# Where three block products of a cross-attention output projection accumulate, and where their weights and the rows behind them are split

## The chip, the cores and the metric

The kernel runs on one core of a Trainium2 chip. The metric is the device time of one execution in microseconds (us); lower is better. The engines that matter here are TensorE (PE in the profile; PEld is its weight load), VectorE (DVE), ScalarE (ACT), GpSimd (POOL) and SyncE (SP), whose queue issues all transfers between device memory and the on-chip memory, SBUF. PE writes its results into PSUM, eight banks of 128 x 512 floats.

## The reference

The kernel computes one layer of an encoder trunk on 1024 tokens of 1024 channels: a mixer (window attention and a gated delta rule side by side), a cross-attention into 256 memory tokens, and a SwiGLU feed-forward. Every sub-layer is wrapped in two RMS norms. What the change touches is the end of the cross-attention and the way into the feed-forward:

```python
    o = jnp.einsum('bhqk,bkhd->bqhd', p, v).reshape(b, s, D_MODEL).astype(h.dtype)
    return o @ w_o
...
        x = x + _rms_norm(c, g_cross_post[l])
        f = _swiglu(_rms_norm(x, g_ffn_pre[l]), w_gate_up[l], w_down[l])
```

All data are float32. A product is made to nearly that precision from three passes: each operand is split into a high part, in the form that PE multiplies at its fast rate (fp32r), and a low part, the rest; PE then adds up high x high, high x low and low x high.

## The kernel before

**Seven products in place of eight.** The projection `o @ w_co` is cut into 2 x 2 blocks: the tokens into a first and a second half of 512, the inner channels into two halves, the output channels into LO and HI. With sums and differences of blocks prepared beforehand, seven block products give the four output blocks (Winograd's form of Strassen's method). One block product is 512 x 512 x 512: 4 tiles of 128 tokens (t), 4 slices of 128 inner channels (k), three passes, so 48 matmuls of 128 x 128 by 128 x 512, all at line 1254 (`three`). `block_product` (line 1256) loops over k outside and t inside and keeps four PSUM banks open.

In order of the program the products are: 1 and 2 into banks A (their sum is the first rows' LO half, copied to `c11`; product 1 alone is kept as `e_`); 3 and 4 into banks Y (`y7 = e_ + Y` in between, `zv = e_ + Y` behind); 5, `part` times b22, into banks X; 6, `s1_` times b11, and 7, `s4_` times a block of w_co, into banks Z. `zv` and `za` are the LO and HI halves of the second rows (together `zl`), `zz` holds the first rows. Before products 6 and 7 the loops are turned: t outside, k inside, so that a tile of rows is complete at every quarter of a product and its finish can begin.

**Weights.** `load_w` (line 119) takes a tile `wraw` from a ring of two, loads it on SP's queue, and splits it into `whi` and `wlo`, two more rings of two: ACT casts the high part (line 103), DVE or POOL subtracts for the low part (line 104). The ring serves all weights of the kernel; the feed-forward's first weights follow those of product 7 in it. `weight_part` (line 1237) splits blocks that are already in SBUF into tiles `wpart`. `part` is a pair of tiles with the split left operand of product 5.

**Finishing a row tile.** `finish` (line 1281), for each of the eight tiles of 128 tokens: load the residual from `d_x1` (SP), the mean square (DVE), its power -0.5 (POOL, 1291), residual added (DVE, 1292), store to `d_x2` (SP), square (ACT, 1295), rstd (POOL, 161 and 162), normalised row (ACT 1299 or DVE 1301, in turn). The adds that take a product from PSUM are at line 1318, the squares at 1279, the multiplications by the gain at 1321 (POOL for LO, DVE for HI).

**Turning the rows.** The feed-forward wants channels in partitions, so PE transposes the normalised rows (line 1379), four 128 x 128 blocks into one bank. For the second half's rows (`first_rows`, in `zl`; the feed-forward takes them first), ACT copies the turned block with its gain from PSUM to `raw` (1390), then ACT casts the high part and DVE subtracts the low part, both from `raw` (1391): `x1h`, `x1l`. The other rows (`last_rows`) are turned the same way and combined with `raw` into four sums T1 to T4 (1402 to 1411). Meanwhile the first four feed-forward blocks run their products on `x1h` and `x1l` alone (1431 to 1447, the matmuls at 1424 under the name pA); the main loop (from 1518) needs T1 to T4.

**What sets the order.** The program is written in one order, and a planner orders each engine's instructions by a simulated time: whatever is ready, the earliest in the program first. Instructions under `high_priority(AHEAD)` count as 300 places earlier; all splits of weights and of left operands do. On the chip each engine then runs its list strictly in that order, and SP's queue too. A tile's memory is given on when its last reader is done: `e_` shares its memory with the first half of `x1h`, `part` with the second halves of `x1h` and `x1l`, and `xr45` (two residual tiles) with the first half of `x1l`.

Of the kernel before, what the change touches and what calls it, by code (L numbers as in the profile page):

```python
# [10 lines left out]
F32 = mybir.dt.float32  # L11
# [65 lines left out]
def tile_hybrid_block(  # L77
# [16 lines left out]
    def f32(ap):  # L94
        return ap.bitcast(F32)
# [1160 lines left out]
    def block_product(banks, a, b_, first=True, last=True, extra=None):  # L1256

        for k in range(HK):
            if k % 2 == 0:
                ah, al = act_part(a, k)  # L1260
            if isinstance(b_, tuple):
                if k % 2 == 0:
                    rows, c0 = (HK * b_[0] + k) * P, HALF * b_[1]
                    wh, wl = load_w(w_co[rows:rows + 2 * P, c0:c0 + HALF], 2, HALF)
                dh, dl = wh[:, k % 2], wl[:, k % 2]
            else:
                dh, dl = weight_part(b_, k)
            for t in range(4):
                three(banks[t], ah[:, k % 2], al[:, k % 2], dh, dl, slice(t * P, (t + 1) * P), first and k == 0,
                      last and k == HK - 1, first and last)  # L1270
            if extra:
                extra(k)
# [33 lines left out]
    def four(spec):  # L1306
        return [p_.tile([P, HALF], F32, tag=t_, name="pst") for p_, t_ in spec]
# [31 lines left out]
    for t in range(4):  # L1339
        square_of(c11[:, t], 0, t)  # L1340
        gained(zz[:, t, LO], c11[:, t], LO)
        add(zv[:, t], e_[:, t], Y[t])
    X = four([PX] * 2 + [PN] * 2)
    block_product(X, tuple(part), b22)
    for t in range(4):
        add(zv[:, t], zv[:, t], X[t])
        square_of(zv[:, t], 0, 4 + t)
        gained(zv[:, t], zv[:, t], LO)
        add(za[:, t], y7[:, t], X[t])
        add(e_[:, t], e_[:, t], X[t])  # L1350
    xr45 = opB3.tile([P, 2, D], F32, tag="b30", name="xr45")
    Z = four([PG] * 4)
    acts = [act_part(s1_, k) for k in (0, 2)]
    wts = [weight_part(b11, k) for k in range(HK)]
    for t in range(4):
        for k in range(HK):
            three(Z[t], *(h[:, k % 2] for h in acts[k // 2]), *wts[k], slice(t * P, (t + 1) * P), k == 0, False, False)
        add(za[:, t], za[:, t], Z[t])
        square_of(za[:, t], 1, 4 + t)
        gained(za[:, t], za[:, t], HI, nc.vector)  # L1360
        finish(4 + t, zl[:, t], (nc.scalar, nc.vector)[t % 2])
    acts = [act_part(s4_, k) for k in (0, 2)]
    wts = [load_w(w_co[(HK + k) * P:(HK + k + 2) * P, HI], 2, HALF) for k in (0, 2)]
    for t in range(4):
        for k in range(HK):
            three(Z[t], *(h[:, k % 2] for h in (*acts[k // 2], *wts[k // 2])), slice(t * P, (t + 1) * P), False, k == HK - 1, False)
        add(zz[:, t, HI], e_[:, t], Z[t])
        square_of(zz[:, t, HI], 1, t)
        gained(zz[:, t, HI], zz[:, t, HI], HI, nc.vector)
        finish(t, zz[:, t], (nc.scalar, nc.vector)[t % 2])  # L1370
    LG.close()

    x1h, x1l = operand(opB, "s1")
    X11, X21 = (x1h[:, 0:HK], x1l[:, 0:HK]), (x1h[:, HK:KT], x1l[:, HK:KT])

    def turned_k(parts, k):
        pt = pn.tile([P, 512], F32, tag="pn", name="ptn")
        for j in range(4):
            nc.tensor.transpose(pt[:, j * P:(j + 1) * P], parts(j, k), ident)
        return pt  # L1380
# [5 lines left out]
        return zz[:, j, k * P:(k + 1) * P]  # L1386

    for k in range(KT):
        pt = turned_k(first_rows, k)
        nc.scalar.activation(raw[:, k, :], pt, AF.Identity, scale=gain("ffn", k))  # L1390
        split(x1h[:, k, :], x1l[:, k, :], raw[:, k, :], eng=nc.vector)
    tr = LR2.enter_context(pool("tr", 1, side="right"))
    T2, T4 = (blocks(t) for t in operand(opA, "s0"))
    T1, T3 = (blocks(t) for t in operand(opB, "s2"))
# [363 lines left out]
```

## Time and profile before

| | us |
|---|---|
| median of 3 runs | 1535.39 |
| lowest and highest of them | 1530.17, 1535.72 |
| the profiled execution | 1530.07 |
| its span | 1528.2 |
| PE busy in the span | 1474.8 |
| DVE, ACT, POOL busy | 1110.1, 745.4, 384.5 |
| all 336 matmuls of the seven products, first to last start | 760.1 to 861.4 |

The span is the part of an execution that the profile covers; the time of the execution is a little longer. A row of a timeline gives the start in the span, the length, engine, line, operation, what is written from what, how many such instructions stand together, and in square brackets how long the engine had stood idle before and what released it. One instruction's length overlaps the next one's start a little on every engine; the cost of one in a full queue is the distance of two starts. A matmul of 128 x 128 by 128 x 512 lasts 0.39 us and the next one starts about 0.23 us later (48 in 11.04 us).

### The profile page before, as it was taken

To read this page: it belongs to the slowest core of one execution; us is meant where nothing else is said; L and a number is where in the kernel's file an instruction comes from. 1 tells how busy PE (TensorE), PEld (TensorE's weight loads), DVE (VectorE), ACT (ScalarE), POOL (GpSimd) and SP (SyncE) were. 2 spreads that over 40 slices of the span, in tenths; PEclk is the share of its full clock that TensorE was granted. 3 is DMA by queue.
4 is the path that set the end of the run, shared out by engine and by line. 5 is a ranking of instruction groups with operands and counts; after the bars stand their busy time and mean duration, and the time that the engine had idled before them with its cause. 6 is when DMAs were issued, how large, how long until landed. Compare 5 with 4: busy or idle time off the path is not lost.

```text
span 1528.2 us, 21073 instructions
## 1 busy us (share of the span) xinstructions
PE 1474.8 (97%) x7403; PEld 1236.7 (81%) x7403; DVE 1110.1 (73%) x1802; ACT 745.4 (49%) x1524; POOL 384.5 (25%) x396
## 2 busy tenths in 40 slices
PE   6999999999999899999999898999999999999997
PEld 5888888878999778888888677888888888888786
DVE  6868999787889865535389886686876554696665
ACT  5578821457567663555455773323223332454532
POOL 2020221311346103342100603352434332000021
PEclk9999999999999999999999999999999999999999
DMA  6235585857996674432341454343433333953255
GB/s 208 76 110 147 144 196 148 222 163 204 322 307 207 223 247 161 168 108 60 104 141 42 173 185 121 123 136 111 152 124 108 104 104 112 328 195 97 103 177 167
DMA packets 264166, 241.91 MB, mean 158 GB/s; under 512 B 33768, under 2 KB 203645, under 8 KB 264061
## 3 DMA queue, kind: packets, MB, share of 16 engines
q1 hardware_dynamic: 264061, 240.57, 50.2%
q8 instruction: 58, 0.95, 0.3%
q14 instruction: 47, 0.39, 0.1%
HBM read 171.02 MB, written 66.88 MB: 156 GB/s over the span
## 4 chain that ended last, share of the span: by engine, by line
PE 67%; DVE 11%; DMA 10%; ACT 6%; issue 3%; SPq 2%; POOL 1%; DVEq 0%; POOLq 0%; ACTq 0%
PE pD L1424 8%; PE pE L1424 8%; PE pA L1424 7%; PE pcq L261 6%; PE pmg L1068 6%; PE pdX L1615 6%; PE pg L261 4%; PE pB L1424 4%; PE pst L1254 4%; PE pdA L1615 2%; PE psc L809 2%; PE pdD L1615 2%; DVE acc L286 2%; DMA qr<-d_q 1%; DVE wlo L104 1%
## 5 line engine op out<-in xcount | busy, mean ns | idle before, releaser
L103 ACT CAST whi<-wraw 128x1024 fp32r<-128x1024 f32 x98 | 102.8, 1050 | 155.0 <-issue 38.2
L104 POOL TENSOR_TENSOR wlo<-wraw,whi 128x1024 fp32r<-128x1024 f32 x38 | 93.0, 2448 | 183.9 <-ACT whi L103 179.6
L261 PE MATMUL pg<-hlo,whi 128*128 128x512 f32 x352 | 139.2, 396 | 0.0
L261 PE MATMUL pg<-hhi,whi 128*128 128x512 f32 x352 | 138.6, 394 | 0.1
L261 PE MATMUL pg<-hhi,wlo 128*128 128x512 f32 x352 | 138.2, 393 | 0.0
L1424 PE MATMUL pA<-b,whi 128*128 128x512 f32 x352 | 112.3, 399 | 2.7 <-ACT m L1441 2.7
L104 DVE TENSOR_TENSOR wlo<-wraw,whi 128x1024 fp32r<-128x1024 f32 x60 | 76.0, 1268 | 42.3 <-ACT whi L103 39.8
L1424 PEld LDWEIGHTS pA<-b,whi 128*128 128x128 f32 x352 | 66.4, 191 | 16.7 <-ACT m L1441 3.3
L1615 PE MATMUL pdX<-dhl,whi 128*128 128x512 f32 x264 | 76.1, 390 | 1.5 <-ACT dhl L103 0.8
L261 PEld LDWEIGHTS pg<-hhi,whi 128*128 128x128 f32 x352 | 66.1, 188 | 13.4 <-ACT hhi L103 0.3
L261 PEld LDWEIGHTS pg<-hlo,whi 128*128 128x128 f32 x352 | 66.2, 188 | 12.7
L261 PEld LDWEIGHTS pg<-hhi,wlo 128*128 128x128 f32 x352 | 66.2, 188 | 12.7
L1502 POOL TENSOR_TENSOR act<-act,up 128x512 f32<-128x512 f32 x33 | 49.8, 1510 | 94.1 <-DVE up L1501 62.0
L1424 PE MATMUL pA<-b,wlo 128*128 128x512 f32 x176 | 69.3, 395 | 0.5 <-DVE wlo L104 0.5
L103 ACT CAST whi<-araw 128x1024 fp32r<-128x1024 f32 (+1 forms) x36 | 35.3, 981 | 68.8 <-PE pdX L1615 27.6
L104 DVE TENSOR_TENSOR wlo<-araw,whi 128x1024 fp32r<-128x1024 f32 (+1 forms) x36 | 40.7, 1131 | 35.8 <-ACT whi L103 35.7
L1474 POOL TENSOR_TENSOR sr<-wraw 128x512 f32<-128x512 f32 x22 | 30.5, 1387 | 130.3 <-DMA wraw<-in_w_gate_up_dram 130.3
L286 DVE SCALAR_TENSOR_TENSOR acc<-cp,cols,acc 128x1024 f32<-128x1024 f32 x48 | 62.0, 1294 | 0.1
L1649 POOL TENSOR_SCALAR frs<-sq 128x1 f32<-128x1 f32 x8 | 11.9, 1496 | 195.4 <-ACT jk L1634 194.5
L1615 PEld LDWEIGHTS pdX<-dhl,whi 128*128 128x128 f32 x264 | 49.3, 188 | 12.7 <-issue 1.1
L1475 DVE TENSOR_TENSOR sr<-sr,wraw 128x512 f32<-128x512 f32 x22 | 37.8, 1719 | 28.4 <-POOL sr L1474 28.4
L1424 PE MATMUL pB<-s,s1h 128*128 128x512 f32 x176 | 54.4, 390 | 2.0 <-ACT s1h L103 2.0
(470 smaller groups left out, 4268.0 us busy)
## 6 DMA issues: line engine op xcount, KB each, us to landing
wraw<-in_w_gate_up_dram SPq DMA_DIRECT2D x52, 512.0 KB, 3.9
kv<-d_kv SPq DMA_DIRECT2D x32, 512.0 KB, 7.4
wraw<-in_w_in_dram SPq DMA_DIRECT2D x22, 512.0 KB, 4.3
b<-in_w_down_dram SPq DMA_DIRECT2D x20, 512.0 KB, 8.0
araw<-d_as SPq DMA_DIRECT2D x20, 512.0 KB, 3.7
pz<-d_pz SPq DMA_DIRECT2D x32, 256.0 KB, 7.0
wraw<-in_w_ckv_dram SPq DMA_DIRECT2D x16, 512.0 KB, 5.6
wraw<-in_w_out_dram SPq DMA_DIRECT2D x16, 512.0 KB, 3.6
```

What stands on the lines that cost most here:

```text
L103: nc.scalar.copy(hi, src)
L104: (eng or nc.vector).tensor_tensor(lo, src, f32(hi), ALU.subtract)
L261: nc.tensor.matmul(p_, w[:, k, :], ah[a][:, k, :], start=(k == 0 and i == 0), stop=(k == nk - 1 and i == 2))
L286: nc.vector.scalar_tensor_tensor(acc, cp[:, t:t + S], taps[t], acc, ALU.mult, ALU.add)
L809: nc.tensor.matmul(out[:, d, h, :], lt[:, d, h, :], rt[:, d, h, :], start=True, stop=True)
L1068: nc.tensor.matmul(pp[t], act[a][:, k, tt], w_[:, kk, :], start=(k == 0 and i == 0), stop=(k == KT - 1 and i == 2))
L1254: nc.tensor.matmul(bank, a[:, tt], w, start=(start and i == 0), stop=(stop and i == 2), skip_group_check=not check)
L1424: nc.tensor.matmul(out_, w[a][:, k, :], xx[b_][:, k, :], start=(start and k == 0 and i == 0), stop=(k == HK - 1 and i == 2), skip_group_ch ...
L1474: nc.gpsimd.tensor_tensor(s[0], b_[:, 0:HK], b_[:, HK:], ALU.add)
L1475: nc.vector.tensor_tensor(s[1], s[0], a_[:, 0:HK], ALU.subtract)
L1502: nc.gpsimd.tensor_tensor(o_, o_, up, ALU.mult)
L1615: nc.tensor.matmul(banks[t], a[:, k - k0, tt], w, start=(first and k == 0 and i == 0), stop=(k == NB - 1 and i == 2), skip_group_check=not ...
```

## The change

Three edits, all between product 5 and the feed-forward.

- Product 6 and product 7 no longer have banks of their own (Z). They accumulate onto product 5 in the four banks X. The two adds of X into `za` and `e_` behind product 5 are gone; `zv` still takes X behind product 5 alone, and after product 6 `za` is `y7 + X`, after product 7 the first rows' HI half is `e_ + X`. The banks are named in another order (PN first, then PX).
- Product 7's weights are loaded into two `wraw` tiles as before, but split into the two `part` tiles, which product 5 has read, instead of `whi` and `wlo` of the ring.
- The second rows, turned, go into banks of PN and PX by turns. They are split straight from PSUM with the gain in both steps (ACT, then DVE at line 107), and POOL makes `raw` from the two parts.

```diff
-    X = four([PX] * 2 + [PN] * 2)
-    block_product(X, tuple(part), b22)
+    X = four([PN] * 2 + [PX] * 2)
+    block_product(X, tuple(part), b22, last=False)
     for t in range(4):
         add(zv[:, t], zv[:, t], X[t])
         square_of(zv[:, t], 0, 4 + t)
         gained(zv[:, t], zv[:, t], LO)
-        add(za[:, t], y7[:, t], X[t])
-        add(e_[:, t], e_[:, t], X[t])
-    xr45 = opB3.tile([P, 2, D], F32, tag="b30", name="xr45")
-    Z = four([PG] * 4)
-    acts = [act_part(s1_, k) for k in (0, 2)]
-    wts = [weight_part(b11, k) for k in range(HK)]
-    for t in range(4):
-        for k in range(HK):
-            three(Z[t], *(h[:, k % 2] for h in acts[k // 2]), *wts[k], slice(t * P, (t + 1) * P), k == 0, False, False)
-        add(za[:, t], za[:, t], Z[t])
-        square_of(za[:, t], 1, 4 + t)
-        gained(za[:, t], za[:, t], HI, nc.vector)
-        finish(4 + t, zl[:, t], (nc.scalar, nc.vector)[t % 2])
-    acts = [act_part(s4_, k) for k in (0, 2)]
-    wts = [load_w(w_co[(HK + k) * P:(HK + k + 2) * P, HI], 2, HALF) for k in (0, 2)]
-    for t in range(4):
-        for k in range(HK):
-            three(Z[t], *(h[:, k % 2] for h in (*acts[k // 2], *wts[k // 2])), slice(t * P, (t + 1) * P), False, k == HK - 1, False)
-        add(zz[:, t, HI], e_[:, t], Z[t])
...
+    def by_tile(a, w, last, then):
+        for t in range(4):
+            for k in range(HK):
+                three(X[t], *(h[:, k % 2] for h in a[k // 2]), *w[k], slice(t * P, (t + 1) * P), False, last and k == HK - 1, False)
+            then(t)
+
+    def row_end(z, r):
+        square_of(z[:, HI], 1, r)
+        gained(z[:, HI], z[:, HI], HI, nc.vector)
+        finish(r, z, (nc.scalar, nc.vector)[r % 2])
+
+    def second_rows(t):
         add(za[:, t], y7[:, t], X[t])
+        row_end(zl[:, t], 4 + t)
+
+    def first_half_rows(t):
+        add(zz[:, t, HI], e_[:, t], X[t])
+        row_end(zz[:, t], t)
+
+    by_tile([act_part(s1_, k) for k in (0, 2)], [weight_part(b11, k) for k in range(HK)], False, second_rows)
+    with tc.high_priority(AHEAD):
+        for k in (0, 2):
+            wr = wp.tile([P, 2, HALF], F32, tag="wraw", name="wraw")
+            nc.sync.dma_start(wr, w_co[(HK + k) * P:(HK + k + 2) * P, HI].rearrange("(k p) n -> p k n", p=P))
+            split(*(t[:, k:k + 2] for t in part), wr)
+    by_tile([act_part(s4_, k) for k in (0, 2)], [[t[:, k] for t in part] for k in range(HK)], True, first_half_rows)
...
-        pt = turned_k(first_rows, k)
-        nc.scalar.activation(raw[:, k, :], pt, AF.Identity, scale=gain("ffn", k))
-        split(x1h[:, k, :], x1l[:, k, :], raw[:, k, :], eng=nc.vector)
+        pt = turned_k(first_rows, k, (PN, PX)[k % 2])
+        split(x1h[:, k, :], x1l[:, k, :], pt, gain("ffn", k))
+        nc.gpsimd.tensor_tensor(raw[:, k, :], f32(x1h[:, k, :]), f32(x1l[:, k, :]), ALU.add)
```

More of the change, by code (lines that the diff above doesn't have):

```diff
@@ L1374, in tile_hybrid_block, with turned_k @@
     X11, X21 = (x1h[:, 0:HK], x1l[:, 0:HK]), (x1h[:, HK:KT], x1l[:, HK:KT])
-    def turned_k(parts, k):
-        pt = pn.tile([P, 512], F32, tag="pn", name="ptn")
+    def turned_k(parts, k, at=PN):
+        pt = at[0].tile([P, 512], F32, tag=at[1], name="ptn")
         for j in range(4):
```

4 lines of the change are left out of this document (1 added, 3 removed).

## The prediction

> **What bounds the kernel now.** I read the page first, then the busy time by stretch around the changed stage, then the waits of PE, and last each engine in order of time. The page:
>
> ```profile
> span 1528.2 us, 21073 instructions
> PE 1474.8 (97%) x7403; PEld 1236.7 (81%) x7403; DVE 1110.1 (73%) x1802; ACT 745.4 (49%) x1524; POOL 384.5 (25%) x396
> PE 67%; DVE 11%; DMA 10%; ACT 6%; issue 3%; SPq 2%; POOL 1%; DVEq 0%; POOLq 0%; ACTq 0%
> ```
>
> PE is the bound of the whole. No matmul is added or taken away, so the change can be worth only what PE loses in its own stage. The stretches, with the columns as the first row names them (PEclk, behind POOL, is the granted clock):
>
> ```profile
> core 0: us, PE busy (x) PEld busy (x) DVE busy (x) ACT busy (x) POOL busy (x), PEclk, DMA share, GB/s
> 826.20:839.80 13.60, 13.60 (x61) 11.26 (x60) 13.60 (x22) 8.90 (x16) 0.21 (x1) 1.00 0.35 116
> 839.80:861.60 21.80, 21.80 (x97) 17.92 (x97) 21.39 (x36) 11.14 (x28) 18.36 (x16) 1.00 0.35 133
> 861.60:867.10 5.50, 0.82 (x5) 0.34 (x4) 4.43 (x6) 5.50 (x10) 2.15 (x6) 0.89 0.34 112
> 867.10:873.00 5.90, 5.43 (x20) 4.27 (x21) 5.20 (x11) 5.73 (x12) 1.99 (x3) 0.53 0.94 297
> 873.00:879.00 6.00, 6.00 (x34) 4.99 (x33) 3.65 (x6) 6.00 (x12) 2.05 (x4) 1.00 0.66 246
> 879.00:888.00 9.00, 7.67 (x36) 5.41 (x34) 6.33 (x7) 8.03 (x13) 2.62 (x4) 1.00 0.64 247
> 888.00:920.80 32.80, 32.76 (x154) 26.65 (x154) 29.16 (x42) 22.50 (x38) 0.00 (x0) 1.00 0.55 176
> 920.80:929.40 8.60, 4.61 (x12) 3.12 (x12) 4.89 (x8) 2.78 (x6) 3.33 (x2) 0.80 0.13 48
> ```
>
> Three things are to be seen. PE is full to 861.6, where the seventh product ends, and then does 0.82 us of work in 5.5. After that hole it runs 5.9 us at a clock of 0.53. And in the two stretches before the hole DVE is full too (13.60 of 13.60, 21.39 of 21.80): the stage is late because of DVE. PE in order of time names who ended the hole:
>
> ```profile
> 839.84 11.04 PE L1254 MATMUL pst<-wpart,b 128*128 128x512 f32 x48
> ...
> 861.60 0.38 PE L1379 MATMUL ptn<-ident,zl 128*128 128x128 f32 x2
> 862.61 0.44 PE L1379 MATMUL ptn<-ident,zl 128*128 128x128 f32 x2 [0.62 <-DVE zl L1301]
> 867.15 1.12 PE L1379 MATMUL ptn<-ident,zl 128*128 128x128 f32 x4 [4.11 <-ACT zl L1299]
> ...
> 922.83 0.73 PE L1424 MATMUL pA<-b,whi 128*128 128x512 f32 x2 [2.07 <-ACT m L1441]
> ```
>
> The transposes wait for the four finished second rows (zl). Why these are late stands in DVE's order:
>
> ```profile
> 839.12 1.21 DVE L104 TENSOR_TENSOR b<-oraw,b 128x1024 fp32r<-128x1024 f32 x1
> 840.26 1.28 DVE L104 TENSOR_TENSOR wpart<-wco,wpart 128x512 fp32r<-128x512 f32 x2
> 841.46 0.67 DVE L1318 TENSOR_TENSOR zl<-zl,pst 128x512 f32<-128x512 f32 x1
> 842.06 0.67 DVE L1318 TENSOR_TENSOR zl<-wco,pst 128x512 f32<-128x512 f32 x1
> ...
> 848.64 1.87 DVE L1318 TENSOR_TENSOR zl<-zl,pst 128x512 f32<-128x512 f32 x3
> ...
> 863.48 1.22 DVE L104 TENSOR_TENSOR wlo<-wraw,whi 128x1024 fp32r<-128x1024 f32 x1 [0.33 <-ACT whi L103]
> ```
>
> Twelve adds on X run from 841.46 to 848.64, 0.60 us apart. The first tile of the sixth product was done at a quarter of its 11.04 us (839.84 + 2.8 = 842.6), but its add came at 848.64, 6 us late. Later two weight splits of the feed-forward stand between the rows' steps.
>
> **The change part by part.**
>
> *Eight adds fall away.* In place of za = y7 + X and then + Z, and of e_ + X and then + Z, one add each remains: 8 x 0.60 = 4.8 us of DVE, all in the full stretch. The second rows then start as each tile of the sixth product ends. The last is done at 839.84 + 11.0 = 850.9; behind it lie an add, a square, a gain, the power on POOL, the residual, a square, rstd and the norm. From 850.9 to 867.15, where PE got the rows, this took 16.2 us in a crowded queue; I put it at 8 to 10 us, which ends at 859 to 861, before the seventh product does. The whole hole goes: 0.62 + 4.11 = 4.7 us, and with it the slow clock behind it, 5.9 x (1 - 0.53) = 2.8. **-7.5 us**. If DVE stays late by half, it is -3.7.
>
> *The same four banks.* This adds a wait. The sixth product now accumulates onto X, so its first matmul waits until zv has taken X[0]. In the trace that add starts at 841.46, behind the splits of the sixth product's own operands, and ends at 842.1, while PE was ready at 839.84: 2.3 us. Least is 0, if the add (X[0] is complete 9 matmuls, 9 x 11.04/48 = 2.1 us, ahead of the product's end) goes first; most is 4.6, if the two new splits of the last weights go ahead of it as well (below, 2 x 1.14). The later banks need theirs 2.8 us apart, and the adds come 0.60 apart, so they cost nothing. Who stands behind PE's wait is everything of the sixth product. A hole also costs clock. The stretch after the 2.07 us hole of 922.83:
>
> ```profile
> 924.00:926.00 2.00, 2.00 (x7) 1.51 (x6) 0.00 (x0) 0.01 (x1) 1.04 (x1) 0.50 0.16 59
> 926.00:928.00 2.00, 1.43 (x4) 0.61 (x2) 0.53 (x1) 0.00 (x0) 0.00 (x0) 0.67 0.00 0
> ```
>
> A hole of 2 us was followed by half speed: 2 x 0.5 + 0.6 x 0.33 = 1.2 us. So 2.3 + 1.2: **+3.5 us** (0 to 4.6 + 2.8 = 7.4, the upper end with the clock loss of the long hole). [...]
>
> *Last weights outside the ring.* The two loads of 512 KB are still issued in their place. Their splits move from before 800 us, where they were hidden, to after the fifth product, which reads the same tiles (part). The rows for this and the next part, grouped over 826 to 930 us, then the two queue rows:
>
> ```profile
> L104 DVE TENSOR_TENSOR wlo<-wraw,whi 128x1024 fp32r<-128x1024 f32 x8 | 9.8, 1221 | 1.3 <-ACT whi L103 1.3
> L103 ACT CAST whi<-wraw 128x1024 fp32r<-128x1024 f32 x8 | 8.3, 1044 | 3.7 <-PE pA L1424 3.7
> L1390 ACT ACTIVATE oraw<-ptn,cols 128x512 f32<-128x512 f32 x8 | 5.5, 700 | 0.2 <-PE ptn L1379 0.2
> L103 ACT CAST b<-oraw 128x512 fp32r<-128x512 f32 x8 | 4.8, 625 | 0.0
> L104 DVE TENSOR_TENSOR b<-oraw,b 128x512 fp32r<-128x512 f32 x8 | 5.4, 686 | 1.2 <-ACT b L103 1.2
> L1403 DVE SCALAR_TENSOR_TENSOR r<-ptn,cols,oraw 128x512 f32<-128x512 f32 x4 | 3.0, 744 | 0.0
> L1321 POOL TENSOR_TENSOR zl<-zl,gpost 128x512 f32<-128x512 f32 x4 | 5.1, 1314 | 0.0
> 787.98 9.87 SPq L126 DMA_DIRECT2D wraw<-in_w_gate_up_dram  x2
> wraw<-in_w_gate_up_dram SPq DMA_DIRECT2D x52, 512.0 KB, 3.9
> ```
>
> DVE gets 2 x 1.14 = 2.3 us (1.22 long, next start 1.14 on) and ACT 2 x 1.0 at 841 to 844, needed at 850.9 plus the wait: covered by the sixth product. In SP's queue the first feed-forward loads, issued at 787.98, now wait for these splits, to some 844; the residual loads queued behind them wait too. They land 3.9 us later, at 848. Their own splits no longer wait for the seventh product to free whi and wlo, so ACT's 2 x 1.0 and DVE's 2 x 1.14 leave the stretch 862 to 867, where they stood in the rows' chain (863.48 above), for about 849 to 852. That gain is already in the -7.5. If the loads come late, ACT stands in front of the rows' squares: up to +4, taken at 0.
>
> *Split from PSUM.* ACT loses 8 casts (8 x 0.51 by spacing = 4.1 us), DVE's eight lo get 744 instead of 686 ns (+0.5), and POOL gets 8 adds at 1.31 = 10.5 us, which nothing but the last rows' first subtraction reads. A bank is now held for ACT and then DVE (0.6 longer), but four banks turn instead of two. ACT was full from 861.6 to 879 (17.23 of 17.40), so its relief reaches PE: from 879 to 888 PE idles 9.00 - 7.67 = 1.3 us. **-1.3 us** (0 to -2.7, that twice over). Against it: POOL's adds stand ahead of the small rstd steps of the first rows (one in progress delays a step by up to 1.3), and may block DVE:
>
> ```profile
> L1475 DVE TENSOR_TENSOR sr<-sr,wraw x22: 683/1768/1778, 928.1 to 1268.1; 128x512 f32<-128x512 f32 x22
> ```
>
> This add, with both inputs in SBUF and POOL adding beside it, takes 1768 ns where it needs 683. The adds of 842 to 848, one input in PSUM, stayed at 0.67 with POOL at work. So the lo splits are safe, and the four residual steps and three gains of the first rows are not: 7 x 1.1 = 7.6 us at most, 0 at least. They have about 43 us of feed-forward products as cover; I charge **+0.6**. [...]
>
> **Sum:** -7.5 + 3.5 - 1.3 + 0.6 = -4.7 us. The profiled execution took 1530.07 us (1.87 around its span), so 1525.4 for one like it. The three runs shown are 1530.17, 1535.39 and 1535.72; the profile stands 5.3 below their median. Against the median: 1535.39 - 4.7 = **1530.7**. A change within 0.5% (7.7 us) can hardly be told from none here.
>
> **The rivals.**
>
> *The handover is free.* DVE takes zv[0] before the later splits, PE starts the sixth product at once. Then -7.5 - 1.3 + 0.6 = -8.2: 1527.2. For it: X[0] is complete 2.1 us early. Against it: from 826.2 to 839.8 DVE has no idle moment, and it took all splits first.
>
> *The wait is the long one (slower).* If the two splits of the last weights and those of the operands all go ahead of zv[0], PE stands 4.6 us and loses 2.8 of clock; with the rows delayed as much, only half the old hole goes (-3.7), and POOL's lock takes its 7.6 where DVE is full: 4.6 + 2.8 - 3.7 + 7.6 - 1.3 = +10: 1545. It decides from a start of the sixth product some 4 us after the fifth ends.
>
> *It does nothing.* DVE works 29.16 of 32.80 us from 888 to 920.8 on the turned last rows. If these start no earlier, PE's gain is handed back before the main loop, at the 2.07 us hole and the one behind it: 1535.
>
> **How the numbers follow.** Forecast 0.40 (1530.7, own range 1526 to 1535), free handover 0.30, long wait 0.16, nothing 0.14. The free handover straddles the 0.5% line and runs beyond it if holes after 879 close as well; with the lower part of the forecast I put faster at 0.35, slower at 0.15, within at 0.50. The range: from 1522, the free handover less one of the bounds (-2.7 for -1.3, no lock) and the lower level of the runs, to 1541, inside the long wait.
>
> **What would show it.** PE's first matmul of the main loop, before:
>
> ```profile
> 929.47 0.74 PE L1424 MATMUL pB<-s,s1h 128*128 128x512 f32 x2 [2.03 <-ACT s1h L103]
> ```
>
> No idle above 1 us between the seventh product and the first feed-forward product, and a clock of 1.00 there; a wait of PE for zv by about 2.3 us at the start of the sixth product; four X adds fewer in two groups; first feed-forward splits before 855; L1475-like lengthened gains while POOL adds. I am wrong if the sixth product starts without a wait, if zl is still awaited after the seventh, or if the main loop does not start some 5 us sooner after the fifth product than the 89.6 us (929.47 - 839.84) of before.

## The result, and the profile after

The changed kernel takes 1543.88 us (median of 8 runs, 1538.55 to 1551.07) against 1535.39 (median of 8, 1530.17 to 1537.56): 1.0060 times as long, 95% interval 1.0037 to 1.0082. It is slower, by some 9 us, and lies above the predicted range (1522 to 1541). The page of the profiled execution (1538.55 us):

```profile
span 1536.8 us, 21068 instructions
PE 1476.0 (96%) x7403; PEld 1238.5 (81%) x7403; DVE 1106.2 (72%) x1794; ACT 743.3 (48%) x1516; POOL 402.9 (26%) x404
PE 63%; DVE 10%; DMA 7%; ACT 5%; issue 3%; POOL 2%; SPq 2%; DVEq 0%; POOLq 0%; ACTq 0%
```

The work changed as announced: DVE has 8 instructions fewer, ACT 8 fewer, POOL 8 more, PE the same. To see where the time went, product 1's first matmul is taken as zero, since the start of that matmul alone wanders by some 10 us between executions of kernels that are alike up to there (760.1 to 770.8 us in the profiles of this study). From it four stretches are measured: to the start of product 5's last matmul, to the end of product 7, to the first feed-forward product, and to the first matmul of the main loop. Busy times by stretch, in columns as in the prediction, before:

```profile
760.10:839.60 79.50, 78.59 (x393) 65.44 (x392) 68.31 (x119) 42.20 (x90) 0.01 (x1) 1.00 0.31 102
839.60:861.40 21.80, 21.80 (x98) 18.02 (x96) 21.39 (x36) 11.14 (x28) 18.36 (x16) 1.00 0.34 129
861.40:870.60 9.20, 4.05 (x19) 2.65 (x17) 7.42 (x13) 9.03 (x18) 4.29 (x9) 0.74 0.59 191
870.60:929.50 58.90, 53.47 (x243) 42.25 (x241) 46.53 (x64) 41.81 (x70) 8.05 (x11) 0.95 0.53 180
sum 169.40, PE 157.91 PEld 128.37 DVE 143.66 ACT 104.18 POOL 30.72; mean PE 39.48 PEld 32.09 DVE 35.91 ACT 26.04 POOL 7.68
```

The same four stretches of the changed kernel:

```profile
761.10:841.50 80.40, 78.91 (x394) 65.52 (x392) 67.72 (x117) 42.51 (x92) 2.06 (x1) 1.00 0.26 89
841.50:866.30 24.80, 22.29 (x98) 17.86 (x96) 17.32 (x24) 10.26 (x24) 16.84 (x12) 1.00 0.45 138
866.30:876.30 10.00, 4.78 (x18) 2.85 (x16) 9.54 (x18) 8.58 (x18) 9.41 (x12) 0.72 0.61 229
876.30:938.60 62.30, 51.91 (x241) 40.67 (x241) 48.91 (x64) 40.10 (x64) 20.09 (x20) 0.97 0.53 176
sum 177.50, PE 157.90 PEld 126.90 DVE 143.50 ACT 101.44 POOL 48.40; mean PE 39.48 PEld 31.72 DVE 35.87 ACT 25.36 POOL 12.10
```

The main loop starts 177.5 us after product 1, before the change 169.4. The stretches grew by 0.9, 3.0, 0.8 and 3.4 us. PE is busy for the same 157.9 us in both, so the 8.1 us are idle time of PE. Taken as length less busy time, it grew by 0.6, 2.5, 0.1 and 5.0 us; the last stretch is only 3.4 longer because PE was also busy 1.6 us less there (51.91 for 53.47, at a clock of 0.97 for 0.95). Behind the start of the main loop both need the same (598.7 and 598.2 us to the end). So all of the loss between these two executions lies in these four stretches. DVE is busy 17.32 of 24.80 us where it was full before: it was relieved, and PE got nothing for it.

PE in order of time, the rows with its longer waits:

```profile
843.06 11.13 PE L1254 MATMUL pst<-wpart,b 128*128 128x512 f32 x48 [1.21 <-DVE zl L1318]
860.92 5.74 PE L1254 MATMUL pst<-part,b 128*128 128x512 f32 x24 [1.30 <-DVE zl L1318]
868.55 0.33 PE L1385 MATMUL ptn<-ident,zl 128*128 128x128 f32 x1 [1.89 <-DVE xr L1292]
871.59 0.69 PE L1385 MATMUL ptn<-ident,zl 128*128 128x128 f32 x2 [2.07 <-DVE zl L1301]
879.36 0.66 PE L1385 MATMUL ptn<-ident,zl 128*128 128x128 f32 x4 [1.82 <-DVE b L107]
887.59 0.33 PE L1385 MATMUL ptn<-ident,zz 128*128 128x128 f32 x1 [1.03 <-DVE b L107]
938.58 1.22 PE L1430 MATMUL pB<-s,s1h 128*128 128x512 f32 x2 [6.24 <-ACT s1h L103]
```

Two handovers of the banks (1.21 and 1.30), the hole behind product 7 still open (1.89 and 2.07 and smaller ones), two waits for the new low part of the turned rows, and a hole of 6.24 us before the main loop, where two of 2.07 and 2.03 were before. This last hole is read from DVE's order of time, the change first, then before:

```profile
936.60 0.68 DVE L104 TENSOR_TENSOR s<-oraw,s 128x512 fp32r<-128x512 f32 x1
937.20 0.68 DVE L1481 TENSOR_TENSOR sr<-sr,wraw 128x512 f32<-128x512 f32 x1
```

```profile
921.54 0.68 DVE L104 TENSOR_TENSOR s<-oraw,s 128x512 fp32r<-128x512 f32 x1
927.47 0.69 DVE L1446 TENSOR_TENSOR sg<-sg,pA 128x512 f32<-128x512 f32 x1 [3.57 <-PE pA L1424]
928.08 0.68 DVE L1475 TENSOR_TENSOR sr<-sr,wraw 128x512 f32<-128x512 f32 x1
```

The main loop's first product needs `s1h`, which ACT makes behind the sum `sr`. Before the change DVE had done the last turned rows' last sum (`s`, 921.54) and then waited 3.57 us for PE's pA; the main loop waited for PE's own products. In the change the last rows come so late that `sr` stands right behind their last sum (936.60), and PE, done with pA at 932.3, waits for DVE.

Why the rows are late again stands in three engines' order. SP's queue, then ACT:

```profile
841.74 0.38 SPq L126 DMA_DIRECT2D wraw<-in_w_gate_up_dram  x1
849.22 1.36 SPq L1288 DMA_DIRECT2D xr<-d_x  x2
850.67 9.99 SPq L126 DMA_DIRECT2D wraw<-in_w_gate_up_dram  x3
```

```profile
857.96 1.05 ACT L103 CAST whi<-wraw 128x1024 fp32r<-128x1024 f32 x1 [9.89 <-DMA wraw<-in_w_gate_up_dram]
```

And DVE:

```profile
847.96 2.31 DVE L104 TENSOR_TENSOR wlo<-wraw,whi 128x1024 fp32r<-128x1024 f32 x1
850.37 1.28 DVE L1318 TENSOR_TENSOR zl<-wco,pst 128x512 f32<-128x512 f32 x2
859.04 1.23 DVE L104 TENSOR_TENSOR wlo<-wraw,whi 128x1024 fp32r<-128x1024 f32 x1 [7.39 <-ACT whi L103]
860.19 0.68 DVE L1318 TENSOR_TENSOR zl<-wco,pst 128x512 f32<-128x512 f32 x1
862.24 0.67 DVE L1318 TENSOR_TENSOR zl<-wco,pst 128x512 f32<-128x512 f32 x1
```

Product 7's weights hold the ring's two `wraw` tiles until DVE has split them, so the second feed-forward load leaves only at 850.67, behind two residual loads that wait for POOL's gains. ACT stands 9.89 us for it, with the second rows' squares behind the cast; DVE stands 7.39 us for ACT, with the sums of the third and fourth second row behind the subtraction. The last of these sums comes at 862.24, although product 6 had ended at 854.2. The wait of 1.30 us in product 7 is this too: its third bank could not be taken over before the sum of 860.19.

### The profile page after: what moved, and what is told of

It reads as the page before. It is cut to its first block, busy times and chain, and to the rows that moved or that the text cites. A ratio compares the mean times of both kernels' runs of the same rounds, so it can differ in the third digit from the quotient of the medians.

```text
span 1536.8 us, 21068 instructions
## 1 busy us (share of the span) xinstructions
PE 1476.0 (96%) x7403; PEld 1238.5 (81%) x7403; DVE 1106.2 (72%) x1794; ACT 743.3 (48%) x1516; POOL 402.9 (26%) x404
## 4 chain that ended last, share of the span: by engine, by line
PE 63%; DVE 10%; DMA 7%; ACT 5%; issue 3%; POOL 2%; SPq 2%; DVEq 0%; POOLq 0%; ACTq 0%
PE pD L1430 8%; PE pE L1430 8%; PE pA L1430 7%; PE pcq L261 6%; PE pdX L1621 6%; PE pmg L1068 4%; PE pB L1430 4%; PE pdA L1621 4%; PE pst L1254 3%; PE psc L809 3%; PE pdD L1621 2%; PE pco L1183 1%; PE pdX L1718 1%; PE pcs L1157 1%; DVE wlo L104 1%
## 5 line engine op out<-in xcount | busy, mean ns | idle before, releaser
L261 PE MATMUL pg<-hhi,wlo 128*128 128x512 f32 x352 | 138.4, 394 | 0.0
```

Of the source, the lines that this page charges most:

```text
L261: nc.tensor.matmul(p_, w[:, k, :], ah[a][:, k, :], start=(k == 0 and i == 0), stop=(k == nk - 1 and i == 2))
```

## The experiments

Each was timed against the kernel before on the same chip; ratios are with 95% intervals. "Main loop" is its start after product 1's first matmul in the one profiled execution of each kernel (169.4 before, 177.5 after).

**The parts.** The shared banks alone, on the kernel before (weights in the ring, turned rows through `raw`):

```diff
-    with tc.high_priority(AHEAD):
...
-    by_tile([act_part(s4_, k) for k in (0, 2)], [[t[:, k] for t in part] for k in range(HK)], True, first_half_rows)
+    acts = [act_part(s4_, k) for k in (0, 2)]
+    wts = [load_w(w_co[(HK + k) * P:(HK + k + 2) * P, HI], 2, HALF) for k in (0, 2)]
+    by_tile(acts, [[t[:, k % 2] for t in wts[k // 2]] for k in range(HK)], True, first_half_rows)
...
-        split(x1h[:, k, :], x1l[:, k, :], pt, gain("ffn", k))
-        nc.gpsimd.tensor_tensor(raw[:, k, :], f32(x1h[:, k, :]), f32(x1l[:, k, :]), ALU.add)
+        nc.scalar.activation(raw[:, k, :], pt, AF.Identity, scale=gain("ffn", k))
+        split(x1h[:, k, :], x1l[:, k, :], raw[:, k, :], eng=nc.vector)
```

> The change with its second and third part undone: products 5 to 7 share the banks X, but product 7's weights go through the ring again and the turned rows are copied by ACT as before. If the late load and POOL's adds make the loss, both are gone: no wait of ACT for the feed-forward weights above 1 us between products 6 and 7, last rows normalised within some 6 us of before, time 1528 to 1536, not slower than before. If the shared banks themselves make it (PE waiting for DVE at the start of products 6 and 7), it stays near the changed kernel, 1541 or more.

Measured: 1.0046 (1.0028 to 1.0063), main loop 176.2. The rival came true: the shared banks are slower by themselves, with no late load and no sums on POOL. PE, then DVE:

```profile
845.88 11.17 PE L1254 MATMUL pst<-wpart,b 128*128 128x512 f32 x48 [2.29 <-DVE zl L1318]
873.66 0.69 PE L1382 MATMUL ptn<-ident,zl 128*128 128x128 f32 x2 [4.70 <-DVE zl L1301]
```

```profile
843.85 1.28 DVE L104 TENSOR_TENSOR wpart<-wco,wpart 128x512 fp32r<-128x512 f32 x2
845.05 2.47 DVE L1318 TENSOR_TENSOR zl<-zl,pst 128x512 f32<-128x512 f32 x4
856.03 1.29 DVE L1292 SCALAR_TENSOR_TENSOR xr<-zl,prs,xr 128x1024 f32<-128x1024 f32 x1 [4.06 <-POOL prs L1291]
857.23 1.28 DVE L1318 TENSOR_TENSOR zl<-wco,pst 128x512 f32<-128x512 f32 x2
862.56 0.67 DVE L1318 TENSOR_TENSOR zl<-wco,pst 128x512 f32<-128x512 f32 x1
```

The handover costs 2.29 us, as the prediction had it. And DVE, which has room now, takes the second rows one by one: the residual sum of the first stands ahead of the sums of the second and third and waits 4.06 us for POOL. The last sum comes 99.0 us after product 1's start, against 90.8 before the change.

The change without the split from PSUM, and the change without the weights outside the ring, the first with the second half of the edit above, the other with its first half:

> The change with only its third part undone (turned rows as before, no adds on POOL). Theory late load: ACT still stands some 10 us for the second feed-forward weights, the second rows come about 7 us late, time at most 3 us under the changed kernel, 1541 to 1544. Theory POOL: the rstd steps of the first rows are free again, PE's hole before the main loop falls from 6.2 to about 2 us, and the time falls by 5 us or more, to 1539 or less.

Measured: 1.0036 (1.0021 to 1.0052), main loop 173.1. ACT, then PE:

```profile
861.38 1.05 ACT L103 CAST whi<-wraw 128x1024 fp32r<-128x1024 f32 x1 [8.60 <-DMA wraw<-in_w_gate_up_dram]
```

```profile
933.51 0.73 PE L1430 MATMUL pA<-b,whi 128*128 128x512 f32 x2 [1.90 <-ACT m L1447]
938.55 0.73 PE L1430 MATMUL pB<-s,s1h 128*128 128x512 f32 x2 [2.03 <-ACT s1h L103]
```

> The change with only its second part undone (product 7's weights in the ring as before). Theory late load: ACT's 9.9 us wait is gone, the second rows are finished before product 7 ends, the hole behind product 7 falls under 2 us, time down by 6 us or more, to 1538 or less. Theory POOL: POOL's adds still hold the rstd steps of the first rows by 3 us each, the hole before the main loop stays at 5 us or more, time within 3 us of the changed kernel, 1541 to 1546.

Measured: 1.0042 (1.0022 to 1.0062), main loop 174.9, no wait of ACT for a load, a hole of 2.03 us before the main loop. Neither expectation holds: without the late load the time is above 1538 (1539.56), without the hole too. So neither alone is the loss. With only the late load taken back the main loop starts 2.6 us sooner than in the change, and the ratio's interval overlaps the change's. Against the shared banks alone (1.0046) the split from PSUM brought nothing that can be told.

**The late load.** The changed kernel, with the second half of product 7's weights in a tile of its own, so that one tile of the ring stays free:

```diff
-            wr = wp.tile([P, 2, HALF], F32, tag="wraw", name="wraw")
+            wr = (wp if k == 0 else tz).tile([P, 2, HALF], F32, tag="wraw" if k == 0 else "wr", name="wraw" if k == 0 else "wr", bufs=None if k == 0 else 1)
```

> The change, but the second half of product 7's weights is loaded into a tile of its own (4 KB per partition) instead of the second place of the ring, so that both feed-forward loads of the first block are issued ahead of the residual loads. Theory late load: ACT waits less than 1 us for them, the second rows come 7 us earlier than in the changed kernel, time down by 5 us or more, 1538 or less. Theory POOL: those rows come earlier but the first rows are still held on POOL and the hole before the main loop stays, time down by 3 us or less.

Measured: 1.0020 (1.0005 to 1.0035), main loop 172.5. ACT has no wait for a load any more. Of the change's 0.60% this edit takes 0.40, some 6 us (5.0 in the profile), and the two intervals just do not meet (1.0035 and 1.0037). The gain isn't in the second rows: these were to come 7 us sooner, and their last norm comes 2.3 us sooner (110.7 for 113.0 after product 1's start), while the wait ahead of product 6 grew to 2.70 us. But the first rows' last norm comes 4.8 us sooner (133.6 for 138.4), DVE's last sum of the turned last rows 4.9 (171.2 for 176.1), and with it the main loop. The hole before it stays at 5.58 us, since DVE is again busy up to it. How much the late load costs depends on what stands beside it: 0.40% here, 0.18% in p13_ring, where it isn't clear of the noise.

**POOL's sums.** The same, with the sums for `raw` on DVE:

```diff
-        nc.gpsimd.tensor_tensor(raw[:, k, :], f32(x1h[:, k, :]), f32(x1l[:, k, :]), ALU.add)
+        nc.vector.tensor_tensor(raw[:, k, :], f32(x1h[:, k, :]), f32(x1l[:, k, :]), ALU.add)
```

> The changed kernel with the second half of the last weights in a tile of its own (as own_tile), and the eight sums of the raw turned rows on DVE in place of POOL. Late load and POOL sums together: with the late load away the own tile gave 1537.5 us and kept a hole of 5.58 us before the main loop; that hole falls to 2 to 3 us and the time to 1533 to 1535 us. Rival, the four shared banks and POOL's gains (eight multiplications ahead of the first power of the closing step of the rows): the hole only moves behind product 7, which again has waits of 3 us or more in sum there, and the time stays at 1536.5 to 1538.5 us.

Measured: 1.0031 (1.0014 to 1.0048), main loop 174.2. PE:

```profile
944.25 1.22 PE L1430 MATMUL pB<-s,s1h 128*128 128x512 f32 x2 [5.58 <-ACT s1h L103]
```

Without a sum on POOL the hole is the same 5.58 us. POOL's sums don't make it.

**POOL's gains.** In the shared-bank kernels POOL's eight gains stand ahead of the first power. The four of the first rows on DVE, on the shared banks alone, on own_dve, and on the kernel before:

```diff
-        gained(zz[:, t, LO], c11[:, t], LO)
+        gained(zz[:, t, LO], c11[:, t], LO, nc.vector)
```

> The four shared banks alone (weights in the ring and turned rows as before the change), with the four gains of the first rows' left half on DVE in place of POOL. Theory, POOL's gains gate the rows: the four on POOL took 6.87 us ahead of the second rows' gains and the first power; on DVE a 128x512 multiplication takes 0.68 us. The first power (line 1291) then starts within 12 us of the first gain of the second rows' left half instead of 12.3 us after POOL's first gain, DVE's idle of 4.06 us before the first residual sum is gone, the 4.70 us hole behind product 7 falls under 2 us, and the time falls from 1541.9 to 1535 to 1538 us. Rival, the handover of the banks (2.29 us of waiting and the clock behind it) and DVE's load: the time stays at 1540 us or more, since DVE gets 2.7 us more work.

> As own_dve, and the four gains of the first rows' left half on DVE. Theory, that late load, POOL's sums and POOL's gains are the three losses and the handover the only one left: 1530 to 1533 us, no hole over 2 us behind product 7 except the turned rows' usual one. Rival, DVE is the bound of this stage: it gets 8 sums and 4 gains more than the changed kernel, 12 x 0.68 = 8.2 us, and the time is 1538 us or more. Rival, the shared banks: 1536 to 1538 us.

> The kernel before, with the four gains of the first rows' left half on DVE in place of POOL. If POOL's gains gate the rows there too (first power at 852.41 us, 12.8 us after POOL's first gain, DVE busy almost all that while): little, 1534 to 1536 us, since DVE has no idle time there before 854 us and gets 2.7 us more. If the gate binds there as in the shared-bank kernels: 1531 to 1533 us. If DVE's load bounds this stage: 1537 to 1539 us.

Measured: 1.0051 (1.0031 to 1.0071), 1.0048 (1.0032 to 1.0065) and 1.0029 (1.0015 to 1.0044); main loop 175.9, 173.6 and 172.2. DVE of p1_gz:

```profile
849.15 5.62 DVE L1321 TENSOR_TENSOR zz<-c,gpost 128x512 f32<-128x512 f32 x4
```

The wait of 4.06 us shrank to 0.73, but the four gains took 5.62 us on DVE beside POOL's own, not 2.7, and the residual sums still came 2.6 to 4.8 us apart. So on POOL the gains seem to hold the first residual sum, but on DVE they cost as much as they free: in all three kernels the time is where the rival had it that counted DVE's load (1541.50, 1539.95 and 1537.22 us). What the rows would do with the gains off both engines is not shown.

**The ring of residual tiles.** A third tile, on the shared banks, on the kernel before, without the weights' part, and on the whole change:

```diff
-            xr = tz.tile([P, D], F32, tag="xr", name="xr", bufs=2)
+            xr = tz.tile([P, D], F32, tag="xr", name="xr", bufs=3)
```

> The four shared banks alone (weights in the ring, turned rows as before the change), with three residual tiles in place of two for the rows that aren't preloaded. New theory, the residual ring: in p1_banks_only row 1's norm stands on DVE behind row 2's residual sum, which waits 4.25 us for its load, and row 3's load (issued 123.6 us after the first product) stands behind that norm; the last row's norm comes 130.9 us after the first product's start (125.6 before the change) and the main loop 45 us behind it. With three tiles row 3's load waits for row 0's norm (113.0) only: last norm by 127 us, the time falls from 1541.9 to 1536 to 1539 us. Rival, the handover of the shared banks (2.29 us) with the slow clock behind product 7 sets the start of the main loop: the residuals come earlier and the time stays at 1540 us or more.

> The kernel before, with three residual tiles in place of two. Residual ring: loads of rows 0 and 1 leave 106.2 and 107.1 us after the first product's start, behind the norms of rows 6 and 7, though the power of row 0 is there at 103.3; with a third tile the load of row 0 leaves before 95 us and the rows end up to 4 us earlier: 1530 to 1533 us. Rival, DVE is full there until 110 us (no idle before the residuals of rows 0 and 1) and sets the rows: 1534 to 1537 us.

> Shared banks and turned rows split from PSUM, raw sums on POOL, weights in the ring, and three residual tiles. Residual ring: last norm falls from 134.2 us after the first product to 128 or less, time from 1539.6 to 1535 to 1537 us. Rival, POOL's eight raw sums hold the square-root steps of the first rows: last norm stays at 131 us or more, time at 1539 us or more.

> The changed kernel, with three residual tiles in place of two. Residual ring: last norm falls from 138.4 us after the first product to 133 or less (the row that comes last had its load issued at 131.4), time from 1543.9 to 1538.5 to 1541 us. Rival, the late load: ACT's wait of 9.89 us ahead of the second rows' squares stays and no residual tile helps against it; with POOL's sums behind it the time stays at 1542.5 us or more.

Measured: 1.0033 (1.0018 to 1.0048), 1.0026 (1.0014 to 1.0039), 1.0062 (1.0047 to 1.0078) and 1.0061 (1.0044 to 1.0077). The last row's norm came sooner in all four (130.9 to 124.3 us after product 1's start, 125.6 to 124.0, 134.2 to 127.9, 138.4 to 130.1), but the main loop only in the first (174.0 for 176.2); in the others it came later (174.0 for 169.4, 176.9 for 174.9, 178.9 for 177.5). On the shared banks alone, before the change and without the weights' part, DVE waits for PE's pA ahead of `sr` (3.45, 3.57 and 3.93 us), so the last row's end doesn't set the main loop's start there. In the change it does, and the third tile shows it: the last sum of the turned rows came at 171.7 for 176.1, the hole of 6.24 us became two of 2.38 and 2.03, and DVE waited 3.54 us for pA. PE was the late one now: its clock in the last stretch was 0.878 for 0.966 in the change, so that (1 - 0.878) x 65.0 = 7.9 us were lost for 2.1. So this theory had the mechanism for the change, and no gain in time.

**Handover and row order.** Product 5's last two depth steps bank by bank, which completes its first bank about 2 us sooner than before, 4 us ahead of the product's end (18 matmuls; with k outside and t inside it is 9, not the 3 of the expectation); and one power for the four second rows, which keeps every residual sum of theirs behind the last of their sums:

```diff
-    block_product(X, tuple(part), b22, last=False)
...
+        for t in range(4):
+            for j in ([k] if k < 2 else [2, 3] if k == 3 else []):
+                three(X[t], *ops5[j], slice(t * P, (t + 1) * P), j == 0, False, False)
```

> The four shared banks alone, with the last two of product 5's four depth steps done bank by bank, so that its first bank is whole 18 matmuls (about 4.1 us) before its last in place of 3 matmuls. Handover theory: the 2.29 us wait ahead of product 6 falls under 0.5 us and the main loop starts 173 to 174.5 us after the first product (176.2 without): 1538.5 to 1540 us. Rival, the rows on DVE set the stage: the wait is gone, the hole behind product 7 grows by as much, and the time stays at 1541 us or more.

```diff
...
+    rs4 = tz.tile([P, 4], F32, name="prs4")
+    nc.vector.scalar_tensor_tensor(rs4, ssq[:, 1, 4:NT], D * EPS, ssq[:, 0, 4:NT], ALU.add, ALU.add)
+    nc.gpsimd.tensor_tensor(rs4, rs4, mhalf[:, 0:4], ALU.pow)
+    for r in range(4, NT):
+        finish(r, zl[:, r - 4], (nc.scalar, nc.vector)[r % 2], rs4[:, r - 4:r - 3])
...
```

> The four shared banks alone, with one power for the four second rows in place of four, so that no residual sum can stand between their sums on DVE. Theory, the row-by-row order: in p1_banks_only the residual sums of the second rows lie 4 to 5 us apart (92.4, 97.0, 99.7, 104.4 us after the first product's start), since each waits on DVE for ACT's square and POOL's power with the next row's sum behind it; before the change they lie 1.2 us apart and end with 98.5. With one power they lie 1.2 us apart, the last at 101 or before, the waits behind product 7 (4.70, 0.56, 0.92 us) sum to 3.5 us or less, and the time is 1538 to 1539.5 us. Rival, the handover alone: 1541 us or more.

> Both at once: the last two depth steps of product 5 bank by bank, and one power for the second rows. If handover and row order are the two losses of the shared banks, main loop 169 to 171 us after the first product and 1533 to 1536 us, as before the change. Rival, TensorE's holes are only moved (each cure gives one back later): 1538 us or more, with its idle time between the first product and the main loop still 15 us or more (11.4 before, 16.1 with the shared banks).

Measured for p1_pair5: 1.0054 (1.0036 to 1.0071), main loop 175.5. PE:

```profile
849.61 3.45 PE L1254 MATMUL pst<-wpart,b 128*128 128x512 f32 x10 [2.29 <-DVE zl L1318]
```

The bank was whole 4 us ahead of product 5's end and the wait stayed 2.29. So it isn't for the last matmuls of product 5, but for DVE, which makes splits for the next products ahead of the sums. Measured for p1_pow4: 1.0038 (1.0020 to 1.0055), main loop 172.8. DVE, then PE:

```profile
857.75 0.69 DVE L1319 TENSOR_TENSOR zl<-wco,pst 128x512 f32<-128x512 f32 x1
861.19 4.87 DVE L1293 SCALAR_TENSOR_TENSOR xr<-zl,prs,xr 128x1024 f32<-128x1024 f32 x4
```

```profile
872.98 1.12 PE L1389 MATMUL ptn<-ident,zl 128*128 128x128 f32 x4 [3.72 <-ACT zl L1300]
```

The order is cured: the last sum at 93.2 us after product 1's start (99.0 before the cure), the residual sums 1.2 us apart. In the profile the main loop starts 3.4 us sooner; the ratios' intervals overlap. Both edits together: 1.0036 (1.0018 to 1.0054), main loop 176.0 with much the same waits as p1_pow4 (2.29 ahead of product 6, 3.72 behind product 7), and a clock of 0.93 for 0.95 in the last stretch. PE's idle time up to the main loop is 16.4 us (11.5 before, 16.1 with the shared banks alone), as the rival had it; the time, 1537.60, lies just under its 1538. Kernels with nearly the same order thus differ by 3 us in a single profile, and no single profile decides on less.

Without the splits' two subtractions on `s1_` (on POOL instead), on p1_pow4:

```diff
-            split(ah, al, a[:, k0:k0 + 2])
+            split(ah, al, a[:, k0:k0 + 2], eng=eng)
...
-    by_tile([act_part(s1_, k) for k in (0, 2)], [weight_part(b11, k) for k in range(HK)], False, second_rows)
+    by_tile([act_part(s1_, k, nc.gpsimd) for k in (0, 2)], [weight_part(b11, k) for k in range(HK)], False, second_rows)
```

> As p1_pow4, with the two low halves of product 6's left operand (2 x 1.22 us on DVE, ahead of the sums that free the banks) on POOL, which is idle until its gains. New handover theory: p1_pair5 left the wait at 2.29 us although the bank was whole 4 us sooner, so the wait is for DVE, whose splits for product 6 (4.7 us) stand ahead of the four sums. With 2.4 us of them on POOL the wait ahead of product 6 falls to 0.7 us or less, products 6 and 7 end about 1.6 to 2.3 us sooner, and the main loop starts 170.5 to 171.5 us after the first product (172.8 in p1_pow4): 1.0015 to 1.0035 times before. Rival, POOL's own slowness: its two subtractions (2.4 us each) come too late for product 6, which waits for them instead: 172.5 us or more and a ratio of 1.0035 or more.

Measured: 1.0017 (1.0006 to 1.0028), main loop 172.8. PE:

```profile
843.63 11.14 PE L1254 MATMUL pst<-wpart,b 128*128 128x512 f32 x48 [1.12 <-DVE zl L1319]
```

The wait was cut by half (0.7 was expected, but of the two subtractions that stand ahead of the sums only one belongs to product 6; the other is product 7's and stayed on DVE). One subtraction less, 1.22 us long, made the wait 1.17 us shorter, so it is DVE's list that the handover waits for. Products 6 and 7 ended 1.2 us sooner than in p1_pow4, but in the profile the main loop started no sooner (172.8 in both), short of the 170.5 to 171.5 expected; the last stretch took 61.6 us for 60.6. So the step in the ratio (1.0038 to 1.0017, the intervals overlapping) is not seen in the profile. With both cures the shared banks went from 1.0046 to 1.0017, the intervals touching at 1.0028.

All cures on the whole change (own tile, sums on DVE, both edits of this part):

> The whole change with all cures: second half of the last weights in a tile of its own, raw sums on DVE, product 5's last two depth steps bank by bank, one power for the second rows. If late load, POOL's sums, handover and row order are the losses: 1531 to 1535 us. Rival, the hole before the main loop (5.58 us in own_dve, with no sum on POOL left) is a loss of its own: it stays over 5 us, and the time is 1536 to 1539 us.

Measured: 1.0037 (1.0020 to 1.0055), main loop 172.0, hole before the main loop 5.58 us. The rival holds.

**No change.** All three parts undone in the changed source:

> The changed kernel with all three parts undone: the same instructions in the same order on every engine as before the change, from other source lines. It tells what part of the losses of 0.2 to 0.6% is the comparison itself. Every theory: ratio 0.999 to 1.001, main loop 169 to 171 us after the first product. If the ratio is 1.002 or more, the losses of own_tile, before_x3 and before_gz are not told from no change.

Measured: 1.0009 (0.9996 to 1.0021). The stretches' sum:

```profile
sum 169.20, PE 157.01 PEld 127.54 DVE 144.89 ACT 104.20 POOL 30.83; mean PE 39.25 PEld 31.89 DVE 36.22 ACT 26.05 POOL 7.71
```

169.2 where the kernel before shows 169.4, in an execution whose product 1 started 10.7 us later and whose engines ran the same instructions in the same order: the measure from product 1 holds. That it holds to 0.2 us is in part luck, since the first stretch is 1.2 us longer here and the last 1.6 shorter (57.3 for 58.9). The run also bounds the ratios: own_tile (1.0020) and p1_pow4_bp (1.0017) can't be told from no change with certainty. No version beat the kernel before.

## Why the prediction was wrong

**"Eight adds fall away", -7.5: 0.** This is the step that failed, and it carried the forecast. It read DVE as full in the two stretches ahead of the hole and took the stage to be "late because of DVE". But DVE was full of work that lay beside PE's. Before the change, in DVE's order of time:

```profile
848.64 1.87 DVE L1318 TENSOR_TENSOR zl<-zl,pst 128x512 f32<-128x512 f32 x3
850.92 0.69 DVE L1318 TENSOR_TENSOR zl<-zl,pst 128x512 f32<-128x512 f32 x1 [0.41 <-PE pst L1254]
```

The last second row's sum (850.92, 90.8 us after product 1's start) came right behind the end of product 6 and waited 0.41 us for PE. Eight adds fewer ahead of it could bring it no more than those 0.41 us. That the earlier sums were late doesn't count, since each bank of turned rows takes a block of all four second rows. And what the step put at "8 to 10 us", from the last sum to PE, is a chain of four rows over DVE, POOL and ACT, where ACT was full before as well (5.50 of 5.50 in the prediction's own row of the hole). With eight adds fewer and the order cured it took 872.98 - 857.75 = 15.2 us in p1_pow4, 16.2 before (867.15 - 850.92). With the order uncured DVE's new room was used to put residual sums ahead of sums (last sum at 99.0). So the hole behind product 7 stayed: 4.9 us after (1.89 + 0.32 + 2.07 + 0.63), 5.1 before (0.62 + 4.11 + 0.35).

**"The same four banks", +3.5.** The wait was right: predicted as 2.3, it was 2.29 where this part stands alone and 1.21 in the whole change. "The later banks cost nothing" was wrong where the sums came late (1.30 in product 7). The clock's 1.2 was not lost here: 1.00 over products 6 and 7 (the last section has the runs where some was).

**"Last weights outside the ring", 0, "up to +4".** Some 6 us in the ratio and 5.0 in the profile by own_tile, 2.6 us in the profile by p13_ring. The step had the mechanism and its price and put both aside, because it let both feed-forward loads leave at 844. Only the first did (841.74). The second needs the second `wraw`, free when DVE had split it (848.04), and then stood in SP's queue behind residual loads that waited for POOL's gains to be done with the memory of `c11`. It left at 850.67 and was there at 857.9, not at 848. The price was paid at the main loop, by the last rows' sums on DVE, and not at the second rows alone. A smaller loss came with it: PE waits 0.93 us for DVE in the attention, 61.8 us after product 1's start, in the three kernels that hold both ring tiles (the change, p12_no_turn, after_x3) and in no other; DVE's list there is in another order once product 7's splits have left it.

**"Split from PSUM", -1.3 and +0.6.** No gain: 1.0042 with it and 1.0046 without. The new order of ACT first, then DVE from the same bank, makes PE wait for DVE (1.82 and 1.03 us). POOL's sums cost nothing that own_dve could give back. No run shows the lock that the range and the long wait's sum name. What the runs show is that some of DVE's instructions took longer beside POOL's: before the change the sum `sr` took 1.76 us at 1010.09, with POOL at work from 1010.01 on, and 0.68 us at 928.08, with POOL idle; in p1_gz four gains took 5.62 us, with POOL at work from 848.93 on.

**The rivals.** The time came within 1.1 us of the long wait's 1545, but by luck: its wait of 4.6 us at product 6 and its lost clock there did not come (1.21 us, clock 1.00), and the loads, to which the sums charged nothing, did. The third rival, "it does nothing", forecast no loss, but had the mechanism of the change's last hole: DVE's work on the turned last rows sets the start of the main loop. Of what the text named as refuting it, two came true: zl is awaited behind product 7, and the main loop starts 96.7 us after product 5 (938.58 - 841.85, where PE fell idle), not 5 us under 89.6.

**What stays open.** The loss isn't a sum of the parts' losses: the shared banks alone already cost 1.0046, with 6.8 of the change's 8.1 us in the profile, and the late load taken back gives 2.6 or 5.0 us. In the five kernels with one hole of 5.6 to 6.4 us before the main loop (the change, own_tile, own_dve, own_dve_gz and own_dve_pow4_5) DVE's sums of the last rows end right ahead of `sr`; all have the three parts, and after_x3, which has them too, has no such hole. Why these sums come so late with all three parts is only traced for the late load. In the other shared-bank kernels PE's own products set the start. There 1.1 to 2.3 us are the handover; why the last stretch is mostly longer (59.1 to 65.0 us, 57.4 in p12_no_turn, for 58.9 before and 57.3 in all_undone) stays open, and it can't be put down to the banks, since before_gz and before_x3, without shared banks, show 60.8 and 61.0. A product 6 with its loops the other way round was not tried.

## What to carry to other kernels

An engine that is full ahead of a hole is the hole's cause only if its last result before the hole is late: look up when the last input was there (here 0.41 us after DVE asked), not how busy the engine is. Where a buffer ring is held longer, follow the next load through its queue, past every load ahead of it and what that one waits for, to the strict list of the engine that splits it; the price stands in front of whatever is queued there. And relief of an engine that a planner orders by simulated times changes the order too: here it let steps with a round trip over two engines in ahead of work that PE was waiting for.

## What the runs showed of the hardware

The prediction charged 1.2 us of clock for a hole of 2 us. Behind the hole of 2.07 us that it took this from, which ended at 922.83 in the kernel before, the granted clock was 0.50 from 923.90 to 927.30, with PE at work all that time: 3.4 x 0.5 = 1.7 us.

The hole ahead of product 6 cost clock in some executions and none in others. With 2.3 us of it the granted clock over products 6 and 7 was 1.00 in four kernels (p1_banks_only, p13_x3, p1_pow4 and p1_pow4_5), and 0.93 in p1_x3 and p1_pair5, whose stretch was 1.5 to 1.7 us longer (25.9 and 26.0 for 24.3 and 24.4). With 2.70 us it was 0.94 in own_tile and 1.00 in own_dve_pow4_5 (26.4 us for 24.8); product 6's 48 matmuls took 12.77 us in own_tile, and 11.13 in p1_gz behind a hole of 2.32. So here such a hole cost some 1.6 us or nothing, and its length does not tell which. What does is not shown.

In p1_gz DVE's four multiplications of 128x512 with both inputs in SBUF took 5.62 us beside POOL's own (1.4 each), where one of the same shape took 0.68 later.
